# Gate-weight sums in a decoder layer on one core: plain copies moved to the output projection, accumulating transfers in quarters over three parts of the MLP

## The chip, the cores and the metric

The kernel runs on one core of a Trainium2 chip. The metric is the device time in microseconds of one execution. TensorE (PE) does the matmuls, VectorE (DVE) and ScalarE (ACT) the elementwise work, GpSimd (POOL) a little elementwise work and its own DMA queue, SyncE (SP) the DMA queue of nearly all loads and stores.

## What is computed

One decoder layer on 512 tokens of width 1024 in float32: attention with a forget gate, a layer norm, a gated MLP with a causal convolution, a second layer norm, and a gated embedding added at the end.

```python
mix = fox_mixer(x, attn_w_in[j], attn_b_f[j], attn_w_out[j])
x = layer_norm(DEEPNORM_ALPHA * x + mix, ln_mix_g[i], ln_mix_b[i])
ffn = conv_ffn(x, ffn_w_up[i], ffn_conv_w[i], ffn_conv_b[i], ffn_w_down[i])
x = layer_norm(DEEPNORM_ALPHA * x + ffn, ln_ffn_g[i], ln_ffn_b[i])
gate = jax.nn.sigmoid(x @ ple_w_gate[i] + ple_b_gate[i])
x = x + gate * (p[i] @ ple_w_proj[i])
```

The change concerns `ple_w_gate`, the 1024 x 1024 weights of the last gate.

## The kernel before, in words

**Precision.** Each float32 operand is cut into a high part (ScalarE, L123) and the low rest (VectorE, L129), and each product is three matmuls: high times high, high times low, low times high (`three`, L152). So every weight block goes from HBM into a `raw` tile (SP, L93, four buffers), is cut into `whi` and `wlo`, and is used by TensorE.

**Fewer products.** Several products, the gate among them, are done on 2 x 2 blocks with seven block products instead of eight (Strassen's scheme in Winograd's form). This needs sums of weight blocks. For the gate, with the blocks b11, b12, b21, b22 of 512 x 512 (1 MB each), they are t1 = b11 + b12, t2 = b22 + t1, t4 = b21 + t2 and t3 = b22 + b12, up to signs that the program puts elsewhere. They are not computed by an engine: four tensors `gt` in HBM receive them by DMA, a block being copied in by a plain transfer and others added to it by accumulating transfers (`accum_op`). Only POOL's queue issues these. The finished tensors are loaded as weights near the end, in `gate`.

**The order of the work.** Attention; then the output projection and the first norm, for each of four tiles `t` of 128 tokens: matmuls into `ap`, `add_half` (VectorE, L654: y becomes alpha y + ps), `half_stats` (L661: statistics of half a row), `norm`. A norm takes the statistics together (L665), adds epsilon (L666), has POOL raise the variance to -1/2 (L667, into `mv`), and scales y in two VectorE instructions; the first needs the mean only (L670), the second needs POOL's result (L671). `flip` transposes a normed tile on TensorE (`nt`, L679) into the next stage's operand `x1h`, `x1l`. Then comes the MLP in four parts over 22 tiles `f` of 128 hidden columns (six in each of the first three parts, four in the last): `up` or `up_step` computes `g` and `u` of a tile, convolution, gelu and product follow, and the down projection of the part before (`x`, `y`, `z`) is interleaved with it. At the end come the rest `r` of the down projection, the second norm, the embedding and the gate (`pl`).

**What places the sums.** `gate_sums` (L261 to L277 before) is a generator. Each step puts a tiny ScalarE instruction as a marker (L271) at that point of ScalarE's order; a tiny POOL COPY reads it (L272), and a DMA is issued behind it on POOL (L274 accumulating, L276 plain). The MLP's loop takes the steps: two at each tile f from 6 to 13. A step moves half a block matrix, 128 x 2 x 512 float32 or 512 KB. POOL's other work there is the six transfers at L126 for weights whose low part is made by DMA, in the tiles before f = 6. VectorE and ScalarE follow an order written by hand from f = 2 on; in the output projection a scheduler sets each engine's order. Each engine executes its own list in order.

Of the kernel before, what the change touches and what calls it, by code (L numbers as in the profile page):

```python
# [13 lines left out]
ALU = mybir.AluOpType  # L14
# [128 lines left out]
def trunk_layer(ctx: ExitStack, tc: tile.TileContext, xT, x2d, pT, wqk, wv0, wv1, wv2, bf, wo, wup, cwb,  # L143
                wdn, wpl, wg, bg, gm, bm, gf, bff, out):
    nc = tc.nc
# [13 lines left out]
    def bank(name, tag=None):  # L159

        tag = tag or next(turns)
        return psum.tile([P, 512], F32, tag=tag, name=name, bufs={"six": 6, "two": 2}[tag])

    def half_rows(w, k0, n, cols):
        return w[k0 * P:(k0 + n) * P, cols * 512:(cols + 1) * 512].rearrange("(k p) c -> p k c", p=P)
# [91 lines left out]
    gq = {f"t{n}": dram.tile([P, 4, 512], F32, name=f"gt{n}") for n in range(1, 5)}  # L257

    steps = itertools.count(16)

    def gate_sums():  # L261
        def quad(g, h):
            src = gq[g] if g in gq else half_rows(wg, 4 * int(g[1]) - 4, 4, int(g[2]) - 1)
            return src[:, 2 * h:2 * h + 2, :]

        for to, src in (("t1", "b11"), ("t2", "b22"), ("t1", "+b12"), ("t4", "b21"), ("t2", "+t1"),
                        ("t3", "b22"), ("t4", "+t2"), ("t3", "+b12")):
            for h in range(2):

                m = next(steps)  # L270
                nc.scalar.activation(small[:, m:m + 1], zeros[:, :1], AF.Copy)  # L271
                with tc.issue_after(nc.gpsimd.tensor_copy(small[:, m + 32:m + 33], small[:, m:m + 1]).ins):  # L272
                    if src[0] == "+":
                        nc.gpsimd.dma_start(quad(to, h), quad(src[1:], h), accum_op=ALU.add)  # L274
                    else:
                        nc.gpsimd.dma_start(quad(to, h), quad(src, h))  # L276
                yield  # L277

    u_up, u_dn = {}, [[] for _ in PAIRS]
    for part in range(4):  # L280
# [3 lines left out]
        for i in range(2 * len(fs)):  # L284
            f, q = fs[i // 2], i % 2
            j, n = f // 2, i % 4
# [6 lines left out]
            for _ in range(CHUNKS[part][i] if part else 0):  # L293
                if todo:
                    src, c, make = todo.pop(0)
# [16 lines left out]
    for g in ("b11", "b21", "t1", "t2", "b22", "t3", "t4"):  # L312
        src = gq[g] if g in gq else half_rows(wg, 4 * int(g[1]) - 4, 4, int(g[2]) - 1)
# [21 lines left out]
    small = base.tile([P, 96], F32, name="neghalf")  # L335
# [233 lines left out]
    def out_first(k):  # L569
        hi, lo = W.get(u_o[0][k // 2])  # L570
        c = slice(k % 2 * 512, k % 2 * 512 + 512)
        for t in range(NT):
            if k == 0:
                acc[t] = bank(f"ao{t}")
            tk = slice(t * P, (t + 1) * P)
            three(acc[t], hi[:, c], lo[:, c], oh[:, k, tk], ol[:, k, tk], k == 0, k == KD - 1,
                  weights_move=True)
# [71 lines left out]
    stats = {}  # L649

    def add_half(t, n, ps, first):
        c = slice(n * 512, (n + 1) * 512)
        if first:
            nc.vector.scalar_tensor_tensor(y[:, t, c], y[:, t, c], ALPHA, ps, op0=ALU.mult, op1=ALU.add)  # L654
        else:
            nc.vector.tensor_add(y[:, t, c], y[:, t, c], ps)

    def half_stats(t, n):
        if n == 0:
            stats[t] = post.tile([P, 2, 6], F32, tag="st", name=f"st{t}", bufs=NT)  # L660
        nc.vector.bn_stats(stats[t][:, n, :], y[:, t, n * 512:(n + 1) * 512])  # L661

    def norm(t, g, b, meanwhile=None):
        mv = post.tile([P, 4], F32, tag="mv", name="mv", bufs=2)
        nc.vector.bn_aggr(mv[:, 0:2], stats.pop(t))  # L665
        nc.vector.tensor_scalar_add(mv[:, 2:3], mv[:, 1:2], EPS)  # L666
        nc.gpsimd.tensor_tensor(mv[:, 3:4], mv[:, 2:3], neghalf, op=ALU.pow)  # L667
        if meanwhile is not None:
            flip(*meanwhile)
        nc.vector.scalar_tensor_tensor(y[:, t], y[:, t], mv[:, 0:1], g, op0=ALU.subtract, op1=ALU.mult)  # L670
        nc.vector.scalar_tensor_tensor(y[:, t], y[:, t], mv[:, 3:4], b, op0=ALU.mult, op1=ALU.add)  # L671
# [34 lines left out]
    g1, b1 = [row(rpool.tile([P, D], F32, name=n), src) for n, src in (("g1", gm), ("b1", bm))]  # L706

    out_first(7)
    for t in range(NT):
        add_half(t, 0, acc[t], True)  # L710
        half_stats(t, 0)
    for t in range(NT):
        ps = bank(f"ap{t}")
        tk = slice(t * P, (t + 1) * P)
        for k in range(KD):
            hi, lo = W.get(u_o[1][k // 2])
            c = slice(k % 2 * 512, k % 2 * 512 + 512)
            three(ps, hi[:, c], lo[:, c], oh[:, k, tk], ol[:, k, tk], k == 0, k == KD - 1,
                  weights_move=True)
            if t > 1 and k == 3:  # L720
                flip(t - 2, x1h, x1l, xt)
        add_half(t, 1, ps, True)
        half_stats(t, 1)
        norm(t, g1, b1, (2, x1h, x1l, xt) if t == 3 else None)
    rows.close()
    oT.close()

# [25 lines left out]
    def product(f, e):  # L753
        a = gates[f]
        nc.scalar.activation(a, a, AF.Gelu)
        nc.vector.tensor_mul(e, gates.pop(f), ups.pop((f, 1)))
# [142 lines left out]
    beside = gate_sums()  # L899
    ordered = ExitStack()  # L900
    for part in range(4):
        ops = []
        slots = iter(CHUNKS[part] or ())

        def between():
            for _ in range(next(slots, 0)):
                next(before)

        for f in range(6 * part, min(6 * part + 6, NF)):
            q, j = f % 2, f // 2  # L910
            if 6 <= f < 14:
                next(beside)
                next(beside)
            if f == 2:

                ordered.enter_context(tc.manual_schedule(
                    engines={mybir.EngineType.DVE, mybir.EngineType.Activation}))
            if q == 0 and j not in APART:
                E = hpool.tile([P, 8 * HALF], F32, tag="E", name=f"E{j}")
            if f == 0:  # L920
                a, b = slice(0, HALF), slice(HALF, S)
                up(0, 0, a)
                up(0, 1, a)
                up(1, 0, a, (3, x1h, x1l, xt))
                up(0, 0, b)
                up(0, 1, b)
                up(1, 0, b)
                conv(0)
                product(0, E[:, :S])
                continue  # L930
            if j in UP_PAIRS:
                if q == 0:
                    up_step(j, 0, 0, E)
                    between()
# [12 lines left out]
                up_step(j, 3, 0, E)  # L947
                up_step(j, 3, 1, E)
                conv_product((f, f - 1), E)
            else:  # L950
                if f > 1:
                    up(f, 0)

                n = 4 * (j - 3 * part) + 2 * q
                late = part and any(sum(CHUNKS[part][:n], i) % 3 == 2 for i in range(CHUNKS[part][n]))
                if not late:
                    conv(f)
                between()
                if late:
                    conv(f)  # L960
                up(f, 1)
                product(f, E[:, q * S:(q + 1) * S])
            if f == 1:
                x_sums()
            if q:
                if part < 3:
                    ops.append([cut_tiles("A", 2, 3, f"a{j}"), cut_tiles("B", 1, 5, f"b{j}", pool=hpool),
                                cut_tiles("S", 4, 4, f"s{j}")])
                    if j + 1 in APART:
                        pending.append(ops[-1])  # L970
                    else:
                        operand_sums(E)
                        operand_parts(ops[-1], E)
                else:
                    h, l = cut_tiles("S", 4, 4, f"s{j}")
                    e = E[:, :2 * S].rearrange("p (a b) -> p a b", b=HALF)
                    last_cut[:] = [nc.scalar.activation(h, e, AF.Copy).ins]
                    nc.vector.tensor_sub(l, e, h.bitcast(F32))
                    ops.append((h, l))
            if j not in UP_PAIRS:  # L980
                between()
        if part < 3:
            before = down(part, ops)
# [37 lines left out]
    b12 = pl[:, tz, 0:512]  # L1021
# [173 lines left out]
```

## Time and profile before

| | |
|---|---|
| median of 3 runs | 652.24 us (651.0 to 653.53) |
| time of the profiled execution | 650.83 us |
| its span, first to last instruction | 649.1 us |
| granted TensorE clock | 1.00 |
| busy share of PE / DVE / ACT / POOL | 99% / 82% / 59% / 18% |
| moved by DMA, mean rate | 121.08 MB, 187 GB/s |

The span is told by views of one profiled execution. A stage table gives the busy time of each engine in a stretch of the span. A wait row says who waited for whom, with the total, the times and the longest wait in us. The chain is the work that ended last, followed back from the last instruction. A timeline row has start, length, engine, line of the kernel before, operation, what is written and read, and in brackets how long the engine had stood idle and what released it; "issue" there means that nothing in the profile is seen to be waited for. Output of a DMA queue has the time from issue to landing.

### The profile page before, as it was taken

The numbers are of one execution on the slowest core, as the hardware profiler recorded it, in microseconds if no ns is written. First come the engines' busy times: TensorE is split into PE (matmuls) and PEld (weight loads), VectorE is DVE, ScalarE is ACT, GpSimd is POOL, SyncE is SP. The second block draws the span as 40 slices with busy tenths as digits, with TensorE's granted clock in tenths as the row PEclk, the third lists the DMA queues.
The fourth block names the chain that finished last, engine by engine and source line by source line (L and its number), as shares of the span: only waits on it lengthen the run. The fifth ranks groups of instructions, "written<-read, shape, count | busy, mean of one in ns | idle before, by whom it ended". The sixth has DMA issues, their size and how long they took to land.

```text
span 649.1 us, 10058 instructions
## 1 busy us (share of the span) xinstructions
PE 639.7 (99%) x3630; PEld 562.6 (87%) x3630; DVE 533.0 (82%) x870; ACT 385.1 (59%) x685; POOL 116.5 (18%) x117
## 2 busy tenths in 40 slices
PE   8999999999999999999999999999999999999997
PEld 7899888888888889889999877999988998888886
DVE  6764779988887599857889798779897998689987
ACT  6553777877785326946657554647555555336873
POOL 0000554454456022110111112300000000002000
PEclk9999999999999999999999999999999999999999
DMA  8764524555598415685696859896545563481372
GB/s 286 245 236 131 204 83 165 172 183 158 181 276 293 151 62 154 130 205 167 205 294 168 228 205 249 248 279 197 197 142 181 162 209 91 156 275 34 126 235 101
DMA packets 49281, 121.08 MB, mean 187 GB/s; under 512 B 4752, under 2 KB 8592, under 8 KB 49232
## 3 DMA queue, kind: packets, MB, share of 16 engines
q1 hardware_dynamic: 45552, 108.92, 51.0%
q0 software_dynamic: 3680, 11.54, 8.9%
q8 instruction: 28, 0.46, 0.3%
q14 instruction: 21, 0.17, 0.1%
HBM read 107.72 MB, written 18.87 MB: 195 GB/s over the span
## 4 chain that ended last, share of the span: by engine, by line
PE 78%; DVE 10%; DMA 6%; issue 2%; ACT 2%; SPq 1%; DVEq 0%; ACTq 0%
PE pp L152 14%; PE g L152 12%; PE u L152 12%; PE pl L152 7%; PE pv L152 7%; PE x L152 5%; DVE wlo L129 4%; PE r L152 3%; PE ap L152 3%; PE o L554 3%; DMA raw<-wdn 2%; PE t L541 2%; PE ao L152 2%; DMA side<-wdn 2%; PE z L152 2%
## 5 line engine op out<-in xcount | busy, mean ns | idle before, releaser
L123 ACT ACTIVATE whi<-raw 128x1024 fp32r<-128x1024 f32 (+4 forms) x141 | 132.3, 944 | 96.1 <-PE pv L152 14.1
L129 DVE TENSOR_TENSOR wlo<-raw,whi 128x1024 fp32r<-128x1024 f32 (+4 forms) x136 | 144.9, 1075 | 27.1 <-ACT whi L123 26.2
L528 POOL TENSOR_SCALAR pr<-pr,rl 128x128 f32<-128x128 f32 (+1 forms) x64 | 75.6, 1196 | 132.6 <-DVE rl L524 132.6
L152 PE MATMUL g<-x1h,whi 128*128 128x256 f32 (+1 forms) x168 | 54.6, 325 | 0.4 <-DVE a L750 0.4
L152 PE MATMUL g<-x1l,whi 128*128 128x256 f32 (+1 forms) x168 | 54.4, 324 | 0.0
L152 PE MATMUL g<-x1h,wlo 128*128 128x256 f32 (+1 forms) x168 | 54.3, 323 | 0.0
L152 PE MATMUL u<-x1h,whi 128*128 128x256 f32 (+1 forms) x160 | 53.0, 331 | 1.2 <-DVE E L821 1.2
L152 PE MATMUL u<-x1l,whi 128*128 128x256 f32 (+1 forms) x160 | 52.9, 331 | 0.0
L152 PE MATMUL u<-x1h,wlo 128*128 128x256 f32 (+1 forms) x160 | 52.9, 331 | 0.0
L152 PE MATMUL pp<-xh,wlo 128*128 128x512 f32 x128 | 50.5, 394 | 0.0
L152 PE MATMUL pp<-xl,whi 128*128 128x512 f32 x128 | 50.0, 391 | 0.0
L152 PE MATMUL pp<-xh,whi 128*128 128x512 f32 x128 | 50.0, 390 | 0.0
L667 POOL TENSOR_TENSOR mv<-mv,neghalf 128x1 f32<-128x1 f32 x8 | 11.6, 1446 | 200.6 <-DVE mv L666 178.3
L520 ACT ACTIVATE pr<-s,nm 128x128 f32<-128x128 f32 (+1 forms) x64 | 33.6, 528 | 9.1 <-DVE nm L516 8.9
L152 PEld LDWEIGHTS g<-x1h,whi 128*128 128x128 f32 x168 | 31.9, 190 | 3.9 <-issue 1.2
L152 PEld LDWEIGHTS g<-x1l,whi 128*128 128x128 f32 x168 | 31.9, 190 | 2.7
L152 PEld LDWEIGHTS u<-x1h,whi 128*128 128x128 f32 x160 | 30.4, 190 | 4.4 <-ACT whi L123 1.4
L152 PEld LDWEIGHTS g<-x1h,wlo 128*128 128x128 f32 x168 | 31.9, 190 | 2.5
L123 ACT ACTIVATE whi<-side 128x512 fp32r<-128x512 f32 (+1 forms) x33 | 25.8, 785 | 13.4 <-DVE side L207 5.4
L152 PEld LDWEIGHTS u<-x1l,whi 128*128 128x128 f32 x160 | 30.4, 190 | 3.0
L152 PEld LDWEIGHTS u<-x1h,wlo 128*128 128x128 f32 x160 | 30.4, 190 | 2.8
L516 DVE CUSTOM_DVE_ANT_0 s<-s,mask 128x128 f32<-128x128 f32 (+1 forms) x64 | 30.0, 512 | 1.7 <-PE s L506 1.5
(629 smaller groups left out, 1848.8 us busy)
## 6 DMA issues: line engine op xcount, KB each, us to landing
raw<-wup SPq DMA_DIRECT2D x34, 512.0 KB, 6.4
raw<-wdn SPq DMA_DIRECT2D x23, 512.0 KB, 3.8
raw<-wqk SPq DMA_DIRECT2D x16, 512.0 KB, 3.4
gt<-wg POOLq DMA_DIRECT2D x12, 512.0 KB, 9.0
ka<-wup SPq DMA_DIRECT2D x8, 512.0 KB, 3.8
kb<-wup SPq DMA_DIRECT2D x8, 512.0 KB
kept<-kb SPq DMA_DIRECT2D x8, 512.0 KB, 3.4
kept<-ka SPq DMA_DIRECT2D x8, 512.0 KB, 3.2
```

The source lines that it names most:

```text
L123: self.nc.scalar.activation(hi[:, c:e], piece, AF.Copy)
L129: self.nc.vector.tensor_sub(lo[:, c:e], piece, hi[:, c:e].bitcast(F32))
L152: nc.tensor.matmul(ps, lhsT, rhs, start=start and n == 0, stop=stop and n == 2, skip_group_check=on)
L516: last_mask[:] = [nc.vector.tensor_tensor_reduce(ps[:, :w], ps[:, :w], mask[:, S - w:], -1.0, BIG, op0=ALU.add, op1=ALU.min, accum_out=nm[ ...
L520: nc.scalar.activation(pr[:, off:off + w], ps[:, :w], AF.Exp, bias=nm[:, i:i + 1], scale=-1.0, accum_out=ls[:, i:i + 1])
L528: nc.gpsimd.tensor_scalar_mul(pr[:, off:off + w], pr[:, off:off + w], rl[:, i:i + 1])
L541: nc.tensor.transpose(ps[:, w:w + P], pr[:, o:o + P], ident)
L554: nc.tensor.matmul(ps[:, q0:], V[:, j, h], p[:, o:o + w], start=j == 0 and n == 0, stop=j == NT - 1 and n == 1)
L667: nc.gpsimd.tensor_tensor(mv[:, 3:4], mv[:, 2:3], neghalf, op=ALU.pow)
```

## The change

The sixteen steps become two generators. `gate_copies` does the eight plain copies (512 KB each) and is driven from the output projection: its marker is a statistics value of the norm, one copy at each of two first halves of rows, two at each of the first three tiles' norms. `gate_sums` keeps the four accumulations, each cut into quarters of 256 KB, and the MLP takes one of these sixteen steps at every tile f from 6 to 21.

```diff
+    def gate_copies():
+        for to, src in (("t1", "b11"), ("t2", "b22"), ("t4", "b21"), ("t3", "b22")):
+            for k in (0, 2):
+                seen = yield
+                with tc.issue_after(nc.gpsimd.tensor_copy(small[:, 48:49], seen).ins):
+                    nc.gpsimd.dma_start(quad(to, k, 2), quad(src, k, 2))
+        yield
+
     def gate_sums():
-        for to, src in (("t1", "b11"), ("t2", "b22"), ("t1", "+b12"), ("t4", "b21"), ("t2", "+t1"),
-                        ("t3", "b22"), ("t4", "+t2"), ("t3", "+b12")):
-            for h in range(2):
+        for to, src in (("t1", "b12"), ("t2", "t1"), ("t4", "t2"), ("t3", "b12")):
+            for k in range(4):
                 m = next(steps)
                 nc.scalar.activation(small[:, m:m + 1], zeros[:, :1], AF.Copy)
                 with tc.issue_after(nc.gpsimd.tensor_copy(small[:, m + 32:m + 33], small[:, m:m + 1]).ins):
-                    if src[0] == "+":
-                        nc.gpsimd.dma_start(quad(to, h), quad(src[1:], h), accum_op=ALU.add)
-                    else:
-                        nc.gpsimd.dma_start(quad(to, h), quad(src, h))
+                    nc.gpsimd.dma_start(quad(to, k, 1), quad(src, k, 1), accum_op=ALU.add)
                 yield
...
     out_first(7)
+    copies = gate_copies()
+    next(copies)
     for t in range(NT):
         add_half(t, 0, acc[t], True)
         half_stats(t, 0)
+        if t % 2:
+            copies.send(stats[t][:, 0, :1])
...
         half_stats(t, 1)
+        st = stats[t]
         norm(t, g1, b1, (2, x1h, x1l, xt) if t == 3 else None)
+        for _ in range(2 if t < 3 else 0):
+            copies.send(st[:, 1, :1])
...
-            if 6 <= f < 14:
-                next(beside)
+            if f >= 6:
                 next(beside)
```

The lists of TensorE, VectorE and SP hold the same instructions in the same order as before. ScalarE's has its sixteen markers singly at the tiles 6 to 21 in place of pairs at 6 to 13. POOL's changes at two places. The first is the output projection; its list of before goes there from the last scaling of probabilities (`pr`) through the four norms to the transfers for `wlo`:

```order
L528 TENSOR_SCALAR pr_2245<-pr_2245,rl_2268 128x384
L528 TENSOR_SCALAR pr_2245<-pr_2245,rl_2268 128x512
L667 TENSOR_TENSOR mv<-mv,neghalf 128x1 x4
L126 DMA wlo_2769<-wup 128x1024
L126 DMA wlo_2899<-wup 128x1024
```

In the changed kernel the lines have moved (the power of a norm is L672, a copy's marker L270 and its DMA L271), `st` is the statistics that a marker reads, and gt_71, gt_72, gt_74 and gt_73 are t1, t2, t4 and t3:

```order
L271 DMA gt_71<-wg 128x2x512
L270 COPY neghalf<-st_2474 128x1
L271 DMA gt_72<-wg 128x2x512
L672 TENSOR_TENSOR mv<-mv,neghalf 128x1
L270 COPY neghalf<-st_2474 128x1
L271 DMA gt_72<-wg 128x2x512
L270 COPY neghalf<-st_2477 128x1
L271 DMA gt_74<-wg 128x2x512
L672 TENSOR_TENSOR mv<-mv,neghalf 128x1
```

So copies 1 to 3 stand ahead of the first tile's power, copies 4 and 5 between the first and the second, and in the same way 6 and 7 ahead of the third and 8 ahead of the fourth. The second place is the MLP. Before, POOL's list runs from the accumulation into t1 over the copy into t4 to the accumulation into t2:

```order
L274 DMA gt_71<-wg 128x2x512
L272 COPY neghalf<-neghalf 128x1
L276 DMA gt_74<-wg 128x2x512
L272 COPY neghalf<-neghalf 128x1
L276 DMA gt_74<-wg 128x2x512
L272 COPY neghalf<-neghalf 128x1
L274 DMA gt_72<-gt_71 128x1024
```

In the changed kernel the last quarter into t1 is followed by those into t2 (marker L280, DMA L281):

```order
L281 DMA gt_71<-wg 128x512
L280 COPY neghalf<-neghalf 128x1
L281 DMA gt_72<-gt_71 128x512
L280 COPY neghalf<-neghalf 128x1
L281 DMA gt_72<-gt_71 128x512
```

The plain copies are gone from here, and each transfer has a quarter of its tensor, 256 KB, with a marker of its own tile ahead of it.

More of the change, by code (lines that the diff above doesn't have):

```diff
@@ L259, in trunk_layer, with quad @@
     steps = itertools.count(16)
[L261 to L268 removed]
+    def quad(g, k, n):
+        src = gq[g] if g in gq else half_rows(wg, 4 * int(g[1]) - 4, 4, int(g[2]) - 1)
+        return src[:, k:k + n, :]
+    def gate_copies():
[5 more added lines that the diff above has]
+        yield
+    def gate_sums():
+        for to, src in (("t1", "b12"), ("t2", "t1"), ("t4", "t2"), ("t3", "b12")):
+            for k in range(4):
                 m = next(steps)
```

## The prediction

> **What bounds the kernel now.** I read the page first, then the busy time by stage, the waits of one stretch, the chain that ended last, and the timelines of POOL and VectorE around the change.
>
> ```profile
> span 649.1 us, 10058 instructions
> ...
> PE 639.7 (99%) x3630; PEld 562.6 (87%) x3630; DVE 533.0 (82%) x870; ACT 385.1 (59%) x685; POOL 116.5 (18%) x117
> ...
> L152 PE MATMUL pp<-xh,whi 128*128 128x512 f32 x128 | 50.0, 390 | 0.0
> ```
>
> TensorE is the bound: only 649.1 - 639.7 = 9.4 us of the span are without a matmul. A change that leaves the matmuls alone can only work on such holes. The stages say which of them lie near the change (columns: length, then busy time of each engine, granted clock, DMA share, GB/s):
>
> ```profile
> 215.00:255.00 40.00, 40.00 (x221) 34.47 (x219) 32.43 (x47) 14.95 (x21) 6.84 (x5) 1.00 0.29 92
> ...
> 318.00:352.00 34.00, 34.00 (x238) 31.84 (x238) 29.82 (x44) 21.35 (x42) 5.49 (x9) 1.00 0.75 236
> 352.00:394.00 42.00, 40.01 (x236) 35.21 (x234) 36.00 (x53) 23.91 (x42) 8.53 (x12) 1.00 0.73 189
> 394.00:432.00 38.00, 37.55 (x229) 33.53 (x228) 28.09 (x39) 20.24 (x35) 8.75 (x12) 1.00 0.94 266
> 432.00:456.00 24.00, 23.89 (x167) 22.21 (x165) 22.52 (x33) 15.85 (x26) 0.00 (x0) 1.00 0.70 213
> 456.00:500.00 44.00, 43.79 (x229) 37.57 (x230) 36.53 (x52) 21.62 (x32) 0.00 (x0) 1.00 0.59 187
> ```
>
> From 318 on, where the gate sums begin, to 500 TensorE is idle 1.99 + 0.45 + 0.11 + 0.21 = 2.76 us. The stretch of the norms, 215 to 255, to which the copies go, has no hole at all, and its DMA share is 0.29 against 0.73 to 0.94. The clock is 1.00 throughout. The waits from 318 to 460 (total, times, longest):
>
> ```profile
> DVE raw L207 <- DMA raw<-wdn: 8.3, 3, 5.2
> DVE side L215 <- DMA side<-wdn: 4.8, 1, 4.8
> PE u L152 <- DVE E L821: 1.2, 1, 1.2
> ```
>
> VectorE waits 8.3 + 4.8 = 13.1 us there for weights, and TensorE's longest wait, 1.2 us, is for VectorE. The chain (start, length, what) leaves TensorE there and runs over those transfers; the last row is the queue list's usual time to landing, and the row ahead of it 24 matmuls at full pace:
>
> ```profile
> 320.77 9.23 DMA raw<-wdn
> ...
> 332.61 6.96 DMA raw<-wdn
> ...
> 366.14 7.99 DMA side<-wdn
> ...
> 427.14 6.20 DMA side<-wdn
> ```
>
> ```profile
> 271.57 5.44 PE g L152 x24
> ```
>
> ```profile
> raw<-wdn SPq DMA_DIRECT2D x23, 512.0 KB, 3.8
> gt<-wg POOLq DMA_DIRECT2D x12, 512.0 KB, 9.0
> ```
>
> Four loads on the path took 9.23, 6.96, 7.99 and 6.20 us where 3.8 is the median: late by 5.4 + 3.2 + 4.2 + 2.4 = 15.2 us. They share the DMA engines with the gate transfers of 9.0 us.
>
> **Part 1: lighter traffic in the MLP.** Before, sixteen transfers of 512 KB (8.4 MB) are issued at tiles 6 to 13. After, eight accumulating quarters of 256 KB (2.1 MB) are left in these tiles, a quarter of the traffic; eight more stand in the following eight tiles. What can be won is bounded by the holes. A matmul is counted busy for 390 ns, but at full pace one starts every 5.44 us / 24 = 227 ns, so each hole is shown about 0.16 us too short; four stages have at least four holes, I count five: 2.76 + 0.8 = 3.6 us. The other end is nothing, if VectorE's own work keeps the holes open. I take three quarters of 3.6, as the traffic falls by three quarters and each hole is smaller than the VectorE wait ahead of it (1.2 against 4.8 us): **-2.6 us**. With these waits gone, what is late next is VectorE's own order (36.00 busy of 42.00 us from 352 to 394), so I don't take it all.
>
> The eight quarters of the later tiles meet a stretch whose holes are 0.21 us from 456 to 500; the loads there have a DMA share of 0.59 around them. Cost between 0 and 0.5 us (the 0.45 of the busiest stage, 394 to 432); I take 0. ScalarE issues sixteen markers as before, eight of them later. The last quarter is issued at tile 21 and first needed by the gate's loads:
>
> ```profile
> 555.03 5.44 PE g L152 x24
> ```
>
> ```profile
> 595.36 0.34 SPq L93 DMA_DIRECT2D raw<-gt  x1
> ```
>
> That is 40 us for a transfer of 9.0 us, and t3, the last one summed, is loaded later still. The quarters stand behind nothing on POOL in the MLP; POOL's only other work there, six transfers for `wlo`, comes ahead of them. No cost.
>
> **Part 2: eight copies in front of the norms.** POOL computes each norm's `mv` (L667 before), and VectorE waits for it. Now three copies are queued ahead of the first `mv`, two ahead of each later one. Their cost on POOL, from the sums' own instructions: the COPY's duration (min/median/max in ns), the time to landing of the eight plain copies at L276, and four issues in a row:
>
> ```profile
> L272 POOL COPY neghalf<-neghalf x16: 201/635/1196, 318.5 to 421.0; 128x1 f32<-128x1 f32 x16
> ```
>
> ```profile
> DMA to landing us min/median/max: 5.6/8.7/11.9
> ```
>
> ```profile
> 352.02 1.19 POOL L274 DMA_DIRECT2D gt<-wg  x1
> ...
> 360.37 1.17 POOL L274 DMA_DIRECT2D gt<-wg  x1 [6.69 <-issue]
> ...
> 361.97 0.72 POOL L276 DMA_DIRECT2D gt<-wg  x1
> ...
> 370.44 0.70 POOL L276 DMA_DIRECT2D gt<-wg  x1 [7.57 <-issue]
> ```
>
> One step (COPY and plain DMA) is 0.64 + 0.71 = 1.35 us, bounded by 0.20 + 0.70 = 0.90 and 1.20 + 0.72 = 1.92. But the queue has a limit: behind one accumulation the next is held 6.69 us, about its landing time; beside one a plain copy is taken at once, a second is held 7.57 us. My estimate from these rows: an accumulation takes two places, a copy one, and there are three. So copy 4 waits for copy 1 to land, copy 5 for copy 2.
>
> Now the norms, by VectorE, POOL and the chain:
>
> ```profile
> 225.42 1.28 DVE L661 BATCH_NORM_STATS2 st<-y 128x6 f32<-128x512 f32 x2
> ...
> 227.80 1.28 DVE L661 BATCH_NORM_STATS2 st<-y 128x6 f32<-128x512 f32 x2
> ...
> 230.84 0.69 DVE L661 BATCH_NORM_STATS2 st<-y 128x6 f32<-128x512 f32 x1
> ...
> 235.54 0.69 DVE L661 BATCH_NORM_STATS2 st<-y 128x6 f32<-128x512 f32 x1
> ...
> 236.58 1.27 DVE L670 SCALAR_TENSOR_TENSOR y<-y,mv,g 128x1024 f32<-128x1024 f32 x1
> 238.30 1.28 DVE L671 SCALAR_TENSOR_TENSOR y<-y,mv,b 128x1024 f32<-128x1024 f32 x1 [0.45 <-POOL mv L667]
> ...
> 244.89 1.28 DVE L671 SCALAR_TENSOR_TENSOR y<-y,mv,b 128x1024 f32<-128x1024 f32 x1
> ...
> 253.26 1.28 DVE L671 SCALAR_TENSOR_TENSOR y<-y,mv,b 128x1024 f32<-128x1024 f32 x1
> ```
>
> ```profile
> 232.28 1.31 POOL L667 TENSOR_TENSOR mv<-mv,neghalf 128x1 f32<-128x1 f32 x1 [22.30 <-issue]
> 236.74 1.52 POOL L667 TENSOR_TENSOR mv<-mv,neghalf 128x1 f32<-128x1 f32 x1 [3.16 <-DVE mv L666]
> 242.78 1.45 POOL L667 TENSOR_TENSOR mv<-mv,neghalf 128x1 f32<-128x1 f32 x1 [4.52 <-DVE mv L666]
> ```
>
> ```profile
> 247.09 0.87 PE nt L679 x8
> ...
> 255.16 0.87 PE nt L679 x8
> ```
>
> - Tile 0: copy 3 starts when its statistics end, 230.84 + 0.69 = 231.5, and POOL is free at 232.9 against 232.28: VectorE, which waits for `mv` and has nothing else in its order, is 0.7 us late (0.2 to 1.2 with the step's ends).
> - Tile 1: its `mv` stands behind copies 4 and 5. Copy 5's statistics end at 235.54 + 0.69 + 0.7 = 236.9; with 1.35 us `mv` starts at 238.3 against 236.74. This `mv` ended 0.41 us behind VectorE's L670 (238.26 against 237.85), so part of its 1.52 us is a wait that now passes under the copies. VectorE is 0.7 to 1.6 us late in all; if copy 2, issued at 227.80 + 1.28 + 0.64 = 229.7, lands only 8.7 us later, at 238.4, copy 5's issue (0.71) and `mv` (0.4 to 1.5) end it 1.3 to 2.4 late. I take **1.6 us**.
> - Tile 2: L671 starts at 244.89, `mv` ended at 244.23; this 0.66 us covers the last step's delay, so the shift stays 1.6. L671 ends at 246.17 + 1.6 = 247.77, where TensorE's transposes stood at 247.09: a hole of 0.7.
> - Tile 3: L671 ends at 254.54 + 1.6 = 256.14; the transposes, now at 255.86, wait 0.3 more.
>
> In short the hole is the shift less 255.16 - 254.54 = 0.62: **+1.0 us**, bounded by 0 and 1.8. The rule that bears here: the Trainium skill, GPSIMD Engine Reference, section Specifications, says that POOL shares its SBUF interfaces with VectorE and contends with VectorE instructions that have two SBUF inputs. The 0.41 us just named agrees; by the rule each COPY that meets a norm's VectorE work lasts toward its 1.2 us, 0.56 more at two norms, and the sum below would be -0.5 us where by the rows' medians it is -1.6.
>
> **The sum.** -2.6 + 1.0 = -1.6 us. The profiled execution's own time is 650.83 us, 1.73 above its span: it becomes 649.2 (span 647.5). The median of the three runs, 652.24, lies 1.41 above the profiled time; with the same step it becomes **650.6 us**.
>
> **The rivals.**
> - *No relief (0.17).* The holes belong to VectorE (36.00 of 42.00 us busy), or eight more issues delay the loads as much as the bytes saved help; then only part 2 is left: 652.24 + 1.0 = 653.2. For it: TensorE's named releaser is VectorE. Against it: the four late loads. The Trainium skill, DMA: Bandwidth & Descriptors, section Rules for kernel authors, tells one to coalesce small transfers into large ones, which speaks against quarters; here 512 KB took 9.0 us in the median, far over what their bytes alone would take by the loads' 3.8, and no run shows 256 KB.
> - *Full relief, copies free (0.18).* All 3.6 us go, and the copies slip into POOL's idle time (its 6.84 us busy of 40.00 speak for it; three queued ahead of the first `mv` against): 652.24 - 3.6 = 648.6.
> - *The full queue in front of the norms (0.12).* All copies land 11.9 us after issue, the longest time shown. Copy 1, issued at 225.42 + 1.28 + 0.6 = 227.3, holds copy 4 until 239.2, and that one holds copy 7, ahead of tile 2's `mv`, until 251.1. With 0.71 and some 1.0 us for `mv`, L671 starts at 252.8 where it stood at 244.89, ends at 254.1, and TensorE stands 7.0 us from 247.09 on; less 2.6 won that is +4.4, 656.6: slower. With a landing time L the hole is 227.3 + 2L + 1.7 + 1.28 - 247.09 = 2L - 16.8, so it eats the gain of 2.6 from L = 9.7 us on. Against it: the DMA share of 0.29 here, while 8.7 was the median at 0.73 to 0.94.
>
> **How the numbers follow.** The forecast has 0.53. About 0.5% is what a measurement of this kernel can tell from no change: 3.3 us, so 649.0 and 655.5. The forecast and the first rival lie within. Two thirds of the second are faster by more (0.12), with 0.02 of the forecast: 0.14. The third lies between 652.2 (L = 9.7) and 656.6: half of it and 0.03 of the first (if the later quarters cost as well) are slower by more: 0.09. The rest is 0.77. The range runs from 648.2, a little below full relief, to 654.4, the third rival's middle; beyond these lie less than 2 in 10.
>
> **What would show it.** Right: the four named loads land in about 4 to 5 us, VectorE's waits for `wdn` fall from 13.1 to about 3 us, TensorE's idle time from 318 to 500 falls from 2.76 below 1 us, and 215 to 260 shows a hole of about 1 us ahead of the `nt` transposes, with VectorE's L671 behind POOL's `mv`. Wrong: the same holes with the loads on time (VectorE's own), no hole at the norms (copies free), or an issue wait of microseconds on POOL before the second `mv` (full queue).

## The result and the profile after

| | before | after |
|---|---|---|
| median of 6 runs each, same chip | 651.1 us | 648.0 us |
| lowest to highest | 650.15 to 653.53 | 646.81 to 648.36 |
| profiled execution, its span | 650.83, 649.1 us | 648.06, 646.4 us |

The ratio is 0.9944, with an interval of 0.9926 to 0.9962: faster by 0.56%, where the prediction had 0.25% (650.6 from 652.24) and a range that began at 648.2. The forecast of 650.6 was 2.6 us too long, and 1.1 of that lies in its start, which was the median of three runs (652.24, where six have 651.1). From the prediction's own start, 652.24 x 0.9944 = 648.6, which is the time that it gave to its rival "full relief, copies free".

The page of the changed kernel: TensorE's busy time is the same, the span is 2.7 us shorter, and POOL's queue (q0) has more packets and a larger share, where it had 3680 and 8.9%.

```profile
span 646.4 us, 10081 instructions
...
PE 639.4 (99%) x3630; PEld 562.9 (87%) x3630; DVE 533.3 (83%) x870; ACT 384.8 (60%) x685; POOL 121.5 (19%) x133
...
q0 software_dynamic: 4320, 11.54, 10.6%
```

The stages of the prediction's table, in the changed kernel:

```profile
215.00:255.00 40.00, 39.94 (x222) 34.34 (x221) 32.23 (x47) 14.82 (x21) 12.94 (x21) 1.00 0.62 197
...
318.00:352.00 34.00, 34.00 (x240) 31.92 (x239) 31.51 (x46) 22.93 (x41) 3.82 (x6) 1.00 0.72 188
352.00:394.00 42.00, 42.00 (x245) 37.01 (x245) 37.90 (x56) 24.13 (x40) 4.12 (x6) 1.00 0.69 180
394.00:432.00 38.00, 38.00 (x237) 34.36 (x236) 29.49 (x41) 18.41 (x30) 2.91 (x4) 1.00 0.75 208
432.00:456.00 24.00, 24.00 (x168) 22.49 (x167) 22.50 (x32) 16.91 (x31) 2.47 (x4) 1.00 0.63 167
456.00:500.00 44.00, 44.00 (x236) 37.91 (x235) 35.88 (x52) 23.27 (x36) 4.05 (x6) 1.00 0.64 192
```

From 318 to 500 us TensorE has no idle time at all, where it had 2.76 us; and at the norms, where the DMA share rose from 0.29 to 0.62, it has 0.06 us. VectorE's waits for weights from 318 to 460 us:

```profile
DVE side L215 <- DMA side<-wdn: 2.1, 1, 2.1
DVE raw L207 <- DMA raw<-wdn: 2.0, 2, 1.3
DVE raw L215 <- DMA raw<-wdn: 0.9, 1, 0.9
```

They fell from 13.1 to 4.1 us on the two rows that the prediction named, so they are not gone; they have only ceased to reach TensorE. All that TensorE waits for in the whole span is this:

```profile
PE pl L152 <- DVE g22h L1147: 1.3, 1, 1.3
PE warm L333 <- DVE zeros L329: 1.1, 1, 1.1
PE pv L152 <- ACT whi L123: 0.4, 1, 0.4
```

The first row, near 633 us in the gate, is new; it comes back below. POOL at the norms, copies 1 to 5 and the `mv` of the first two tiles (in brackets the idle time ahead):

```profile
226.86 0.93 POOL L271 DMA_DIRECT2D gt<-wg  x1 [0.39 <-issue]
228.50 1.03 POOL L270 COPY neghalf<-st 128x1 f32<-128x1 f32 x1 [0.71 <-DVE st L666]
229.47 0.71 POOL L271 DMA_DIRECT2D gt<-wg  x1
230.94 0.18 POOL L270 COPY neghalf<-st 128x1 f32<-128x1 f32 x1 [0.77 <-DVE st L666]
231.40 0.69 POOL L271 DMA_DIRECT2D gt<-wg  x1 [0.28 <-issue]
232.11 0.76 POOL L672 TENSOR_TENSOR mv<-mv,neghalf 128x1 f32<-128x1 f32 x1
...
235.65 0.18 POOL L270 COPY neghalf<-st 128x1 f32<-128x1 f32 x1 [1.95 <-DVE st L666]
236.89 0.69 POOL L271 DMA_DIRECT2D gt<-wg  x1 [1.06 <-issue]
237.59 0.58 POOL L672 TENSOR_TENSOR mv<-mv,neghalf 128x1 f32<-128x1 f32 x1
```

The queue's limit is there: POOL stands 1.06 us ahead of copy 5, whose issue starts 0.3 us after copy 2 has landed (issued at 229.47, landed after 7.1 us). Some 0.39 us of the 1.06 are no hold, as they stand ahead of copy 1 too, with the queue empty. But six of the eight COPYs last 0.17 to 0.18 us, and in the first three tiles `mv` takes 0.6 to 0.8 us where it lasted 1.3 to 1.5. The time from issue to landing, first of the eight copies, then of the sixteen quarters:

```profile
DMA to landing us min/median/max: 4.9/5.8/7.1
```

```profile
DMA to landing us min/median/max: 4.6/5.7/8.7
```

### The profile page after: what moved, and what is told of

It is laid out like the page before. It is cut to its first block, busy times and chain, and to the rows that moved or that the text cites. A ratio compares the mean times of both kernels' runs of the same rounds, so it can differ in the third digit from the quotient of the medians.

```text
span 646.4 us, 10081 instructions
## 1 busy us (share of the span) xinstructions
PE 639.4 (99%) x3630; PEld 562.9 (87%) x3630; DVE 533.3 (83%) x870; ACT 384.8 (60%) x685; POOL 121.5 (19%) x133
## 4 chain that ended last, share of the span: by engine, by line
PE 91%; DMA 3%; ACT 2%; DVE 2%; issue 1%; SPq 0%; ACTq 0%; DVEq 0%
PE g L152 18%; PE u L152 18%; PE pp L152 14%; PE x L152 8%; PE pv L152 7%; PE z L152 4%; PE r L152 3%; PE ap L152 3%; PE ao L152 3%; PE o L559 3%; PE t L546 3%; PE y L152 2%; PE s L509 2%; PE pl L152 2%; PE s L511 2%; DMA raw<-gt 2%
## 5 line engine op out<-in xcount | busy, mean ns | idle before, releaser
L280 POOL COPY neghalf<-neghalf 128x1 f32<-128x1 f32 x16 | 9.0, 562 | 247.0 <-ACT neghalf L279 247.0
```

## The experiments

Three things were done at once: the copies were moved, the accumulations were spread over more tiles, and they were cut into quarters. The question is which of them removed the holes and what the copies cost at the norms. The theory is that accumulating transfers near the first down-projection weights make the holes. The rivals are that the number of bytes of any kind does it, that the size of a piece does it, and that copies at the norms take something back. Each diff is against the changed kernel, save that of spread_16, which is against the kernel before, and that of spread_sum_at_8, which is against spread_16. TensorE, VectorE and SP have the same order in all of these kernels, save that no_sums loads other blocks and copies_twice differs around the norms. Each ratio is to the kernel before, in runs on the same chip.

| kernel | median us | ratio, interval | TensorE idle 352 to 394 us |
|---|---|---|---|
| after_again | 647.41 | 0.9942, 0.9926 to 0.9958 | 0.00 |
| spread_16 | 646.83 | 0.9941, 0.9919 to 0.9963 | 0.00 |
| copies_only | 647.24 | 0.9946, 0.9928 to 0.9963 | 0.00 |
| halves_8_plain | 647.35 | 0.9947, 0.9925 to 0.9969 | 0.00 |
| halves_from_8 | 647.55 | 0.9950, 0.9933 to 0.9966 | 0.00 |
| halves_every_2nd | 647.28 | 0.9952, 0.9937 to 0.9967 | 0.00 |
| spread_sum_at_8 | 647.76 | 0.9961, 0.9946 to 0.9976 | 0.00 |
| halves_8 | 649.04 | 0.9972, 0.9957 to 0.9987 | 0.93 |
| no_sums | 648.52 | 0.9972, 0.9954 to 0.9989 | 0.00 |
| halves_skip_8 | 648.78 | 0.9974, 0.9959 to 0.9988 | 0.66 |
| quarters_8 | 649.21 | 0.9981, 0.9960 to 1.0002 | 1.03 |
| copies_twice (two executions) | 664.80 | 1.0209, 1.0157 to 1.0262 | 0.00 |

All kernels with holes in this stage are near 649 us; those without are at 647 to 648, except two whose loss is elsewhere.

### No sums at all (no_sums)

```diff
-            copies.send(stats[t][:, 0, :1])
...
-            if f >= 6:
-                next(beside)
...
-        src = gq[g] if g in gq else half_rows(wg, 4 * int(g[1]) - 4, 4, int(g[2]) - 1)
+        g0 = {"t1": "b12", "t2": "b22", "t4": "b21", "t3": "b22"}.get(g, g)
+        src = half_rows(wg, 4 * int(g0[1]) - 4, 4, int(g0[2]) - 1)
```

> The gate's sums are left out: no transfer on POOL's queue for them anywhere, and the gate loads plain blocks of the weights in place of t1 to t4, so the output is another one. It bounds what taking the gate transfers out of the MLP can bring. Theory (the holes of TensorE from 318 to 500 exist only because gate transfers delay the weight loads): all of these holes go, TensorE idle there under 0.3 us against 2.76, and no wait of VectorE for POOL at the norms beyond the 0.45 us of before; about 3.5 us under the kernel before, ratio about 0.9945. Rival (VectorE's own work holds part of the holes open): 1 us or more of idle time stays from 352 to 394 and the ratio is about 0.998.

TensorE's idle time from 318 to 500 us is 0.00, so the sums make all of the holes there. The time missed what was expected. In the profiled execution the loss is at the gate, which now loads blocks of `wg` where it loaded `gt`: TensorE stands 2.01 us between 616 and 644 us, and the granted clock is 0.94 there. That the stand-in is the reason is likely, but no run shows it. So the kernel tells of the MLP, and its total of nothing else.

### The copies alone (copies_only)

```diff
-            if f >= 6:
-                next(beside)
```

> The changed kernel without its sixteen accumulating quarters (the output is another one): the eight copies at the output projection alone. Its difference to the run without any sums is the price of the copies at the norms. Theory from the changed kernel's trace (its wait of VectorE for the second norm grew from 0.45 to 1.07 us, the hole in front of the last transposes is 0.2 us): 0.2 to 0.3 us over the run without sums, ratio to before about 0.995. Rival (my prediction's term): a hole of 1.0 us, ratio about 0.996, VectorE's wait at the second norm 1.5 us or more.

Nothing is lost at the norms: from 215 to 260 us TensorE is busy 45.00 of 45.00 us. The ratio agrees with that of the whole change, so the sixteen quarters cost nothing that can be measured, and neither do the eight copies in this execution.

### Halves at eight tiles, quarters at eight tiles (halves_8, quarters_8)

The copies stay at the norms; the accumulations are put back into the tiles 6 to 13, as one half of 512 KB a tile, or as two quarters a tile. The first:

```diff
-            for k in range(4):
+            for k in (0, 2):
...
-                    nc.gpsimd.dma_start(quad(to, k, 1), quad(src, k, 1), accum_op=ALU.add)
+                    nc.gpsimd.dma_start(quad(to, k, 2), quad(src, k, 2), accum_op=ALU.add)
...
-            if f >= 6:
+            if 6 <= f < 14:
```

> The copies moved as in the changed kernel, but the four accumulations in halves of 512 KB, one at each tile from 6 to 13: the copies' part of the change alone, half of the old traffic in these tiles. Theory A (bytes in these tiles decide, holes shrink in proportion): half of the holes stay, 1.0 to 1.8 us of idle time from 318 to 460, ratio about 0.997. Theory B (a hole opens only when the loads are later than VectorE's slack, so half of the traffic is already enough): under 0.5 us idle, ratio about 0.9945, the quarters add nothing. Theory C (the accumulations do the harm): nearly 2.8 us idle, ratio 1.000.

Half of the gain goes (0.28% of 0.56 is left), which is nearest to theory A; but the next runs speak against the bytes. The stage table and the waits of 318 to 460 us of halves_8 show the holes again, and VectorE's long waits for weights.

```profile
352.00:394.00 42.00, 41.07 (x239) 35.90 (x238) 38.07 (x55) 24.68 (x43) 3.49 (x5) 1.00 0.70 184
```

```profile
DVE raw L207 <- DMA raw<-wdn: 7.3, 3, 4.0
DVE side L215 <- DMA side<-wdn: 3.2, 1, 3.2
```

The other only changes the loop, with halves cut in two again:

```diff
-            if f >= 6:
+            if 6 <= f < 14:
+                next(beside)
                 next(beside)
```

> The changed kernel with its sixteen accumulating quarters taken two at each tile from 6 to 13, as many bytes at each tile as the run with halves there: the size of a piece alone. Theory (time on the DMA engines around tiles 8 and 9 decides, not the size of a piece): holes as with the halves, 1 to 2 us in all from 352 to 394, ratio about 0.997. Rival (smaller pieces let the loads through): under 0.5 us, ratio about 0.9945. Third (each further transfer costs time of its own): over 2 us, ratio about 0.999.

It has the same holes:

```profile
352.00:394.00 42.00, 40.97 (x239) 35.86 (x239) 37.63 (x55) 24.79 (x44) 9.14 (x11) 1.00 0.70 177
```

So with the plain copies, half of the bytes, gone from these tiles, holes are left (1.99 us before), and the size of a piece neither mends nor makes them. The Trainium skill (DMA: Bandwidth & Descriptors, section Rules for kernel authors) tells one to coalesce small transfers, and names 64 KB as the size below which they are mostly overhead. Between 256 and 512 KB these two runs show no difference: their intervals overlap.

### Halves without accumulating (halves_8_plain)

```diff
-                    nc.gpsimd.dma_start(quad(to, k, 1), quad(src, k, 1), accum_op=ALU.add)
+                    nc.gpsimd.dma_start(quad(to, k, 2), quad(src, k, 2))
```

This beside the other two edits of halves_8.

> As the run with halves at the tiles 6 to 13, but its eight transfers there are plain copies in place of accumulations (the same bytes, tiles and order; the sums, and so the output, are other ones). Theory (accumulating costs the DMA engines two to three times the time of a plain copy of the same bytes, and that is what delays the loads at tiles 8 and 9): no hole over 0.3 us from 352 to 394 where the accumulations left 1.88 in all, transfers landing in 5 to 6 us against 7 to 10, ratio about 0.9945. Rival (bytes per tile): the holes of the accumulating run stay, 1.0 us or more.

The same tiles and bytes as in halves_8, and no hole. The transfers of L281 to landing, in halves_8:

```profile
DMA to landing us min/median/max: 6.8/8.2/10.2
```

and in halves_8_plain:

```profile
DMA to landing us min/median/max: 4.5/5.5/6.3
```

The packets of queue 0 (count, MB, share of the sixteen engines' time in the stretch) for the two halves of tiles 6 and 7, which read `wg`, from 318 to 340 us, first in halves_8 and then in halves_8_plain:

```profile
q0 software_dynamic: 544, 1.05, 36.0%
```

```profile
q0 software_dynamic: 288, 1.05, 20.2%
```

and for the two of tiles 8 and 9, which read `gt`, from 350 to 370 us:

```profile
q0 software_dynamic: 288, 1.05, 43.5%
```

```profile
q0 software_dynamic: 288, 1.05, 20.2%
```

So the kind of transfer counts: at one half a tile, an accumulated one is too much and a plain one is not. For the same bytes the accumulated halves take about twice the engines' time (1.8 and 2.2 times), and that is so even where the number of packets is the same. The Trainium skill (Collectives: The Full Stack, section The bandwidth ceiling) says of the add in a ReduceScatter that it reads two sources and has two read descriptors a chunk where a copy has one. Twice the time agrees with this; the packets here are doubled only where `wg` is read, so they do not show it.

### The sixteen old steps, spread (spread_16)

The steps of the kernel before, copies and all, in their old order and size, but one at each tile 6 to 21 in place of two at 6 to 13:

```diff
-            if 6 <= f < 14:
-                next(beside)
+            if f >= 6:
                 next(beside)
```

> The kernel before with its sixteen steps of 512 KB, plain and accumulating, taken one at each tile from 6 to 21 in place of two at each from 6 to 13: the spreading alone, no copy at the norms. Theory A (bytes per tile): half of the traffic in each tile, holes of 1.0 to 1.8 us over 318 to 570, ratio about 0.997. Theory B (slack): under 0.6 us idle over 318 to 570, ratio about 0.9945, as the changed kernel. If pairs are what hurts, the same as B. Theory D (the copies' place is what counts): ratio 1.000.

It is as fast as the whole change, with no hole from 318 to 500 us. So neither the move to the norms nor the quarters is needed; the spreading alone is enough. Its first four steps are plain copies. Its accumulations at tiles 10 and 11 landed only after 9.6 to 10.8 us and opened no hole, which says that place matters too.

### Which tiles (spread_sum_at_8, halves_skip_8, halves_from_8, halves_every_2nd)

The first has the sixteen spread steps with each copy followed at once by its accumulation:

```diff
-        for to, src in (("t1", "b11"), ("t2", "b22"), ("t1", "+b12"), ("t4", "b21"), ("t2", "+t1"),
-                        ("t3", "b22"), ("t4", "+t2"), ("t3", "+b12")):
+        for to, src in (("t1", "b11"), ("t1", "+b12"), ("t2", "b22"), ("t2", "+t1"), ("t4", "b21"),
+                        ("t4", "+t2"), ("t3", "b22"), ("t3", "+b12")):
```

> Sixteen steps of 512 KB as in the kernel before, one at each tile 6 to 21, but with each plain copy followed at once by the accumulation that needs it: plain copies at tiles 6 and 7, accumulations at tiles 8 and 9, and so on in turn. The result is the same as the reference's. Theory (lateness of VectorE adds up over tiles 6 to 9, and accumulations have to lie at more than two of them): the two accumulations of tiles 8 and 9 alone open less than 1 us between 352 and 394 us, none near 361 us; time within 0.5 us of the version with all sixteen spread, 646.5 to 647.5. Rival (what lies at tiles 8 and 9 alone decides): about 1.9 us of lost TensorE time between 352 and 394 us, as with the eight halves, and a time near 649.

No hole, with accumulations at tiles 8 and 9 that landed after 8.4 and 8.7 us: the rival, that what lies at tiles 8 and 9 alone decides, falls. The time is 0.3 us above the expected, and this run stood 1.2 us near 633 us. The other three are halves_8 with another loop:

```diff
-            if 6 <= f < 14:
+            if f in (6, 7) or 10 <= f < 16:
```

> The eight accumulations in halves of 512 KB, at tiles 6, 7 and 10 to 15, so that nothing is issued at tiles 8 and 9. The result is the same as the reference's. Theory of place (the weights of tiles 8 and 9 are the ones that VectorE cannot wait for): the 0.9 us of TensorE idleness between 352 and 394 us goes to less than 0.4, a time near 648. Rival (the rate of accumulating bytes anywhere in the MLP): 0.9 us stays, only moved to after tile 10, and the time stays near 649.

Both expectations missed: of 0.93 us 0.66 stayed, but not moved to after tile 10. What stayed is the hole near 361 us, so tiles 8 and 9 are not its place; a wait of 0.2 us near 393 us, which halves_8 has, is gone. Next, the eight halves two tiles later:

```diff
-            if 6 <= f < 14:
+            if 8 <= f < 16:
```

> The eight accumulations in halves of 512 KB, one at each tile 8 to 15, so that nothing is issued at tiles 6 and 7 and the rate behind is as with the halves at 6 to 13. The result is the same as the reference's. Theory (accumulations at tiles 6 and 7 make VectorE late for the first down-projection weights, near 330 and 339 us, and the holes near 361 us are that lateness): no hole near 361, idleness of TensorE between 352 and 394 us under 0.3 us, a time of 647 to 648. Rival (what counts is the number of accumulations in a row, wherever they begin): holes of 0.7 us or more open two tiles later, after 375 us, and the time stays near 649.

The hole near 361 us is gone, at the same rate and piece size: accumulations at tiles 6 and 7 made it. None opened two tiles later either, with no idle time from 352 to 456 us. But this execution stands 0.81 us between 456 and 500 us, behind the last two halves, where VectorE waited 4.1 us for a load; halves_skip_8 has these halves at the same tiles, a wait of 2.2 us there, and no hole. Each has one profiled execution, so whether this late hole belongs to the kernel stays open. Last, one half at every second tile:

```diff
-            if 6 <= f < 14:
+            if f >= 6 and f % 2 == 0:
```

> The eight accumulations in halves of 512 KB, one at every second tile 6, 8, 10 to 20: the same bytes in the same time as the sixteen quarters, in pieces twice as large. The result is the same as the reference's. Theory (VectorE's lateness comes from accumulating bytes per tile): no hole above 0.4 us, a time of 647 to 648, as with the quarters. Rival (a piece of 512 KB is late by itself, so the quarters are what the change needs): the hole of 0.8 us near 361 stays, and a time near 648.5 to 649.

No hole: the quarters are not needed, as long as only one half falls into tiles 6 and 7. VectorE's timeline shows why, with the waits for the first down-projection weights. Before:

```profile
330.03 0.69 DVE L207 TENSOR_TENSOR raw<-raw,side 128x512 f32<-128x512 f32 x1 [1.48 <-DMA raw<-wdn]
339.60 0.69 DVE L207 TENSOR_TENSOR raw<-raw,side 128x512 f32<-128x512 f32 x1 [1.61 <-DMA raw<-wdn]
```

halves_8:

```profile
330.21 0.69 DVE L207 TENSOR_TENSOR raw<-raw,side 128x512 f32<-128x512 f32 x1 [2.18 <-DMA raw<-wdn]
339.30 0.69 DVE L207 TENSOR_TENSOR raw<-raw,side 128x512 f32<-128x512 f32 x1 [1.14 <-DMA raw<-wdn]
```

halves_every_2nd, where the second load comes in time:

```profile
330.20 0.69 DVE L207 TENSOR_TENSOR raw<-raw,side 128x512 f32<-128x512 f32 x1 [2.27 <-DMA raw<-wdn]
```

and after, where only the second is late:

```profile
337.15 0.69 DVE L207 TENSOR_TENSOR raw<-raw,side 128x512 f32<-128x512 f32 x1 [0.72 <-DMA raw<-wdn]
```

VectorE loses 1.48 + 1.61 = 3.1 us and 2.18 + 1.14 = 3.3 us in the two kernels with a hole near 361 us, and 2.3 and 0.7 us in those without. In quarters_8 and halves_skip_8, which have the hole too, it loses 3.1 and 3.4 us. So VectorE can be some 2.3 us late here before TensorE notices, and 3.1 us is too much. TensorE waits 0.7 us in all four, whether 3.1 or 3.4 us were lost, so the runs show that there is a limit, and not how the hole grows beyond it.

The largest hole of the kernel before, the wait of 1.2 us that the prediction shows, is another one, near 377 us. It stands behind the two accumulated halves of tile 8, where VectorE waits 4.8 us for `side`. In halves_8, with one accumulated half at each of the tiles 8 and 9, that wait is 3.2 us and no hole opens near 377 us, so there is a limit here too.

As for the hole near 361 us, the kernel before has no accumulation at tiles 6 and 7. Its four steps there are plain copies, two a tile; those of tile 6:

```profile
319.07 0.79 POOL L276 DMA_DIRECT2D gt<-wg  x1
320.73 0.71 POOL L276 DMA_DIRECT2D gt<-wg  x1
```

So my theory was too narrow. Counted in plain halves, with an accumulated half as two, tiles 6 and 7 have two each in before, halves_8, halves_skip_8 and quarters_8, which have the hole near 361 us, and one on average in after, spread_16, spread_sum_at_8, halves_8_plain and halves_every_2nd, which do not. That count fits all of these; it is a summary of them, and no run tested it at another load.

### Twice as many copies at the norms (copies_twice)

Each plain copy is done twice, the first time into a tensor that nobody reads:

```diff
+                    nc.gpsimd.dma_start(gx[to][:, k:k + 2, :], quad(src, k, 2))
+                seen = yield
+                with tc.issue_after(nc.gpsimd.tensor_copy(small[:, 48:49], seen).ins):
                     nc.gpsimd.dma_start(quad(to, k, 2), quad(src, k, 2))
...
-        for _ in range(2 if t < 3 else 0):
+        for _ in range(4 if t < 3 else 0):
```

> The changed kernel with sixteen copies in place of eight at the output projection, each half copied into a spare tensor as well: four ahead of the first norm's power, four between each two. It tests the limit of the queue in front of the norms. Theory (three copies at a time, a further one waits for a landing of 5 to 7 us, so a copy each 2 to 2.5 us once the queue is full, while 4.5 to 8 us lie between two norms): POOL shows issue waits of over 1 us behind the third copy, the second power comes 3 to 5 us late, and TensorE stands 4 us or more in front of the transposes; time 648 + 4 or more, slower than before. Rival (no such limit, a copy costs POOL 0.9 us): the powers are 2 us later at most, hole under 1.5 us, not slower than before.

This is the rival of the full queue, made real. POOL's timeline, from the fourth copy on:

```profile
234.48 0.70 POOL L275 DMA_DIRECT2D gt<-wg  x1 [3.23 <-issue]
...
258.57 0.70 POOL L275 DMA_DIRECT2D gt<-wg  x1 [3.75 <-issue]
259.28 0.58 POOL L676 TENSOR_TENSOR mv<-mv,neghalf 128x1 f32<-128x1 f32 x1
```

and who waits for that (215 to 318 us):

```profile
DVE y L680 <- POOL mv L676: 16.9, 4, 6.1
...
PE nt L688 <- DVE y L680: 12.0, 2, 7.2
```

With the limit of three reached at every tile, TensorE waits 12 us at the norms. Its busy time is also 4.6 us longer than in the changed kernel (644.0 for 639.4), and the granted clock falls to 0.95 there (last section). The copies of the change are free because their number fits the queue, and only just: copy 5's hold and the hole at the norms go together. In seven executions of kernels with these eight copies POOL stood 0.38 to 0.58 us ahead of it, little more than the 0.39 of an empty queue, and TensorE was busy 45.00 of 45.00 us from 215 to 260; in the changed kernel's first it was 1.06 us, with 0.06 us idle. In halves_from_8 copy 2 happened to land 8.1 us after issue:

```profile
237.78 0.69 POOL L271 DMA_DIRECT2D gt<-wg  x1 [2.05 <-issue]
```

```profile
215.00:260.00 45.00, 44.13 (x255) 38.30 (x254) 36.33 (x53) 17.28 (x26) 12.96 (x21) 1.00 0.65 196
```

One microsecond more of hold, 0.81 us more of hole.

### The change once more (after_again)

> The changed kernel once more, unaltered, beside the others on one chip: a second profile of it. What belongs to the kernel must come again: no hole of TensorE over 0.3 us from 318 to 570, a hole of about 0.2 us in front of the last transposes of the norms. The hole of 1.5 us near 633 us, at the gate's loads, comes again if it is the kernel's, and is of another size if it is that execution's. Ratio to before 0.993 to 0.996.

The same code: 0.9942 against 0.9944, and no idle time from 318 to 500 us. The hole at the norms did not come again (45.00 of 45.00 us busy). The wait near 633 us is 0.7 us here.

## Why the prediction was wrong

- **The sign and the mechanism of part 1 were right.** The loads of `wdn` were late beside the gate transfers, VectorE waited, TensorE waited for VectorE; halves_8 and halves_8_plain show it by bringing the holes back and taking them away.
- **The step that failed: "I take three quarters of 3.6, as the traffic falls by three quarters."** A hole is not in proportion to the traffic. It opens when VectorE's lateness passes its slack, so near 361 us it is gone as soon as the lateness is under some 2.3 us, though 4.1 us of VectorE's waits are left on the two rows above. The term was -2.6 and measured -3.7. The starts of the same matmuls show it, here the last transposes of the first norm and the first of the second, before:

```profile
255.00 1.04 PE L679 MATMUL nt<-ident,y 128*128 128x128 f32 x8
586.50 1.03 PE L679 MATMUL nt<-ident,y 128*128 128x128 f32 x8
```

and after:

```profile
254.50 1.06 PE L684 MATMUL nt<-ident,y 128*128 128x128 f32 x8
582.27 1.03 PE L684 MATMUL nt<-ident,y 128*128 128x128 f32 x8
```

That is 331.5 us and 327.8 us. So the bound of 3.6 us, with 0.16 us hidden in each of five holes, was right, and all of it went. The sentence that VectorE's own order comes late next also fell: with VectorE as busy as 37.90 of 42.00 us, there is no hole.
- **What in the traffic mattered was put down to the bytes.** The three quarters counted all 8.4 MB alike. The runs show that an accumulated half weighs about like two plain ones, and, for the hole near 361 us, that it is what meets the loads of tiles 6 and 7 that decides: eight plain halves at tiles 6 to 13 leave no hole, eight accumulated ones do, and the same eight from tile 8 on leave none there.
- **Part 2's +1.0 us was mis-sized; it measured 0.06 us (0.2 with the hidden 0.16)**, 0 in seven other executions and 0.87 in one. The mechanism, three places, copy 5 behind copy 2, was right. The step that failed is VectorE's shift of 1.6 us: its wait for the second `mv` grew from 0.45 to 1.07 us, so the shift was 0.6, and by the prediction's own rule, the shift less 0.62, nothing is left:

```profile
238.21 1.29 DVE L676 SCALAR_TENSOR_TENSOR y<-y,mv,b 128x1024 f32<-128x1024 f32 x1 [1.07 <-POOL mv L672]
```

The landing time was taken from rows at a DMA share of 0.73 to 0.94 (8.7 us, partly behind accumulations), and the copies run at 0.62 and land in 5.8. The step was taken with the COPY's median from the MLP, 0.64 us, where six of eight took 0.17 to 0.18 us. And the second `mv`, which ran beside VectorE's L670 before, starts now after that and takes 0.58 us in place of 1.52: the cost that "now passes under the copies" was larger than I allowed.
- **The rule that the prediction takes from the Trainium skill (GPSIMD Engine Reference, section Specifications) held.** The two long COPYs, 1.03 and 0.79 us, each end with a VectorE instruction of two inputs; the first, from 228.50 to 229.53, ends with this one:

```profile
228.28 1.21 DVE L129 TENSOR_TENSOR wlo<-raw,whi 128x1024 fp32r<-128x1024 f32 x1
```

It stands ahead of copy 2, and copy 5 waited for copy 2 to land, so it may have a part in the 1.06 us. The +1.1 us that the prediction gave for such COPYs did not come.
- **The eight later quarters**: nothing, as forecast, with no idle time from 456 to 500 us.
- **The total.** The two parts make -3.7 + 0.2 = -3.5 us, and the spans differ by -2.7. By the starts above, the changed kernel is 0.5 us earlier at the last transposes of the first norm, though the norms cost it 0.2, chiefly by a shorter wait of TensorE for ScalarE in the attention (`pv`, 0.4 us for 1.5 in these executions). Behind the second norm's first transposes it takes 1.5 us more (62.6 and 64.1 us), most of it the 1.3 us near 633 us, which no step foresaw. That wait was 0 in the profiled executions of before, copies_only, halves_8_plain and halves_every_2nd, 0.7 in after_again, 2.0 in no_sums and 0.3 to 1.2 in the others. It comes with and without the copies at the norms and with and without quarters; its cause stays open.
- **The range was too narrow at the fast end.** It stopped at 648.2, though the case of full relief gave 648.6 and the six runs of the changed kernel lie up to 1.5 us apart. What happened is that case, in both of its parts; it deserved more than its 0.18.

## What to carry to other kernels

A hole behind a late load opens only when the lateness passes the slack, so a relief that takes the lateness under the slack takes the whole hole and not a share of it; look for the loads ahead of the hole, and at what is issued beside them. Ask of a transfer what kind it is before counting its bytes: an accumulated half weighed here like two plain ones. Take the time to landing from rows at the DMA load that the moved transfer will meet, and count the places of its queue: up to the limit a copy costs its issue, beyond it what is left of an earlier one's landing time.

## What was not expected of the hardware

- An accumulating transfer of 512 KB in DRAM lands in 6.8 to 10.2 us where a plain one at the same tiles takes 4.5 to 6.3. Its packets take about twice the engines' time, with 272 packets for 144 where it reads `wg` and with the same 144 where it reads `gt`.
- A tiny POOL COPY took 0.17 to 0.18 us in six of eight cases and up to 1.03 us beside a VectorE instruction of two inputs; POOL's power of 128 x 1 took 0.58 us with VectorE idle and 1.52 us beside such an instruction.
- In copies_twice the granted clock fell in the stages with the pauses and behind them, and was back at 1.00 from 318 us on:

```profile
215.00:260.00 45.00, 34.25 (x153) 27.66 (x151) 23.79 (x36) 11.91 (x16) 13.51 (x28) 0.95 0.72 184
260.00:318.00 58.00, 56.72 (x349) 51.83 (x350) 43.16 (x64) 34.53 (x48) 10.21 (x14) 0.95 0.77 203
```
